# An encoder layer on one core: gt1 multiplied into the output weights ahead of the output projection, the second norm's 1/rms on ScalarE, two blocks of these weights kept, the last transposes two blocks earlier

## The chip, the cores and the metric

The kernel runs on one core of a Trainium2 chip. The metric is the device time of one execution in microseconds (us). Before the change three runs took 1608.18, 1610.39 and 1611.52 us; their median is 1610.39. The core's engines are TensorE (PE; its weight loads are shown as PEld), VectorE (DVE), ScalarE (ACT), GpSimd (POOL) and SyncE (SP). SP issues the DMAs; "SPq" in the profile is its queue. Each engine works through its own list of instructions in order, and the engines wait for one another through semaphores.

## The reference

One layer of an encoder on 1024 tokens of width 1024, in float32:

```python
h = rms_norm(x, g_norm1) * (1.0 + sc1) + sh1
proj = h @ w_in                       # q, k, v of two branches, and the gates
...                                   # neighbourhood attention -> o_a, dilated attention -> o_b
gate_a, gate_b = split(sigmoid(gates + b_gate))
merged = gate_a * (o_a @ w_proj_a) + gate_b * (o_b @ w_proj_b)
x = x + gt1 * (merged @ w_o)

h2 = rms_norm(x, g_norm2) * (1.0 + sc2) + sh2
a, up = split(h2 @ w_ffn_in)
x = x + gt2 * ((silu(a) * up) @ w_ffn_out)
```

Here `rms_norm(x, g) = x * rsqrt(mean(x*x) + eps) * g`. The six rows sh1, sc1, gt1, sh2, sc2, gt2 (1024 numbers each, the same for all tokens) come from the conditioning vector, `silu(c) @ w_ada + b_ada`. The change works on the line with gt1, on the norm behind it and on the start of the FFN. As gt1 scales columns, `gt1 * (merged @ w_o)` is also `merged @ (w_o * gt1)`.

## The kernel before

**Arithmetic.** Each float32 operand of a large matmul is split into two float32r parts, hi (a copy on ScalarE) and lo (the operand minus hi, a subtraction on GpSimd or VectorE). Three matmul passes (`PASS`: hi·hi, hi·lo, lo·hi) make one product. A matmul covers 128 x 128 x 512. So each weight tile of 128 x 512 costs a load, an ACT copy (`whi`, line 101) and a subtraction (`wlo`, line 102).

**Rings.** All weights go through `raw`, a ring of 6 buffers of 256 KB, filled by `wload` (line 94) from SP's queue. `wsplit` (lines 97 to 103) turns a raw buffer into one buffer of each of the rings `hi` and `lo`, 10 each. A buffer of a ring is filled again when all readers of its last content are done, and SP, which issues loads and stores in one list, stands at an instruction until that is so.

**Stages** (times in the profiled run): projection and attention to about 640 us; gates and merge, 641 to 829; output projection, 829 to 936; FFN in, 936 to 1400; FFN out, to the end.

*Gates and merge* (lines 882 to 900). Eight column blocks i. `gates(i, br)` makes the two sigmoid gates of a block (96 matmuls, weights `wg`), `merge(i)` the two projections and `mg = gate_a*pa + gate_b*pb` (36 matmuls, weights `wpa`, `wpb`; the VectorE lines 837 to 839). The gates of blocks 0 to 3 are already there when the loop starts, so merges 0 to 3 run back to back from 669 to 708 us, and from then on gates(i) and merge(i) take turns. In the same loop `w2_combos(k)` prepares the later FFN-out weights: four loads (`in_w` in the profile's names, which leave digits out), four dependent additions or subtractions, two on GpSimd and two on VectorE (lines 875 to 878), and four stores to DRAM (line 880, `w_d<-raw`). `W2C` says after which merge which of them are written. They use the same six raw buffers.

*Output projection* (lines 968 to 985, `SWEEPS`). Three sweeps, over the token tiles 0 to 2, 3 to 5 and 6, 7. A sweep goes over eight k blocks; for each block both halves of `wo` are loaded and split, `m` (hi and lo of the merged block, lines 963 and 964) is made, and 18 (12 in the last sweep) matmuls run. Operands are made two steps ahead (`AHEAD`). After a sweep's last block `o_post(t)` works on each tile: VectorE multiplies the product by the row gt1 (line 927) and adds it to x (line 930); ScalarE squares it with a sum (line 931); `rstd` (lines 108 to 118) makes 1/rms by ScalarE's Ln and Exp and a correction step in small VectorE operations (lines 933, 113, 115, 116, 117); VectorE scales the tile (line 935) and GpSimd adds sh2 (line 936). `o_turn(t)` (lines 939 to 950) transposes the tile on TensorE and splits it to `h2T`, the operand of the FFN. The turns of a sweep's tiles are written into the next sweep (`TK`), those of tiles 6 and 7 behind ffn1(HT, 0).

*Start of FFN in* (lines 1116 to 1130). `ffn1(j, hf)` is 48 matmuls into two PSUM banks. Four of them run first, (0,0), (HT,0), (0,1), (HT,1). The other blocks are made in pairs with seven products instead of eight (p1 to p7); for that `make_t` (lines 1036 to 1050) prepares sums and differences of `h2T` for all tiles, mostly on VectorE. p1, p2 and p3 of the first pair need no result of make_t; p6 is the first that does.

**What sets the order.** TensorE's order is the program's. For ScalarE, VectorE, GpSimd and SP the order after the start of the kernel is set by a scheduler from the program's dependences and its own costs; so an instruction that is added in one place can shift those of other lines.

## Time and profile before

| | before |
|---|---|
| median of 3 runs | 1610.39 us |
| profiled execution, of it the span | 1611.13 us, 1609.3 us |
| TensorE busy | 1549.1 us (96%), 8240 matmuls |
| VectorE, ScalarE, GpSimd busy | 1026.0, 667.0, 719.5 us |
| mean granted TensorE clock | 0.984 |
| merges 0 to 3 | 669.0 to 708.3 us |
| gates and merges 4 to 7 | to 829.1 |
| o sweeps 1, 2, 3 | to 861.6, 901.5, 935.6 |
| ffn1(0,0), ffn1(HT,0), turns 6 and 7 | to 960.9 |
| ffn1(0,1), ffn1(HT,1) | to 983.1 |
| p1, p2, p3 and p6 of the first pair | to 1010.4 |

A line of a timeline gives the start, the length, the engine, the line of the code, the operation, output and inputs by name (numbers left out), shapes, and how many instructions follow each other; behind it, in brackets, the idle time of the engine ahead of it and what ended that. A line of the windows gives, for each stretch of time, its length, the busy time and number of instructions of each engine, the granted clock of TensorE, the busy share of the 16 DMA engines and what they moved (GB/s). A line of the waits gives who waited for whom, the sum in us, how often, and the longest.

### The profile page before, as it was taken

The page shows a single profiled execution, that of the slowest core. Times are in us where ns is not written, and L with a number is a line of the kernel's source. Part 1 is how long each engine was busy: PE and PEld are TensorE (multiplying, and loading weights), DVE is VectorE, ACT ScalarE, POOL GpSimd, SP SyncE. Part 2 cuts the span into 40 slices and gives each one's busy share as a digit, 9 for nine tenths or more (in the row PEclk, how much of TensorE's full clock was granted, in tenths as well). Part 3 has the DMA queues.
Part 4 walks back from the last instruction along what each step waited for, and adds up shares of the span by engine and source line. Part 5 has one row for each costly group of instructions (what it writes and reads, how often), then busy time and mean ns, then how long its engine had stood idle before and what let it go on. Part 6 is the DMA issues. An engine that isn't in the chain of part 4 may idle for free.

```text
span 1609.3 us, 24779 instructions
## 1 busy us (share of the span) xinstructions
PE 1549.1 (96%) x8240; PEld 1293.8 (80%) x8240; DVE 1026.0 (64%) x2188; ACT 667.0 (41%) x1734; POOL 719.5 (45%) x672
## 2 busy tenths in 40 slices
PE   7989999999999999999999986999999999999997
PEld 6888888898888877878887775788888888888886
DVE  5666666776889843352437979866666666345476
ACT  5555555555545443512124533323233333344442
POOL 1332321221101040645425576867766666555565
PEclk8999999999999999999999998999999999999999
DMA  8332331344344351776645521333333333576774
GB/s 316 105 119 58 102 110 49 119 133 113 91 133 127 91 172 57 257 236 218 216 152 183 176 93 40 102 111 102 108 109 99 105 98 120 178 232 193 249 216 166
DMA packets 149056, 227.52 MB, mean 141 GB/s; under 512 B 27312, under 2 KB 65072, under 8 KB 148928
## 3 DMA queue, kind: packets, MB, share of 16 engines
q1 hardware_dynamic: 148928, 225.94, 44.1%
q8 instruction: 65, 1.06, 0.3%
q14 instruction: 63, 0.52, 0.1%
HBM read 172.28 MB, written 53.59 MB: 140 GB/s over the span
## 4 chain that ended last, share of the span: by engine, by line
PE 76%; DVE 11%; DMA 5%; issue 3%; ACT 2%; POOL 2%; SPq 0%; POOLq 0%; DVEq 0%; ACTq 0%
PE ps_d L281 14%; PE ps_t L1059 6%; PE ps_v L1059 6%; PE ps_s L1059 6%; PE ps_d L1059 6%; PE ps_d L570 4%; PE ps_d L592 4%; PE ps_s L570 4%; PE ps_d L1161 3%; PE ps_s L1161 3%; PE ps_v L473 2%; PE ps_s L432 2%; PE ps_v L1161 2%; PE ps_t L1161 2%; PE ps_t L570 2%
## 5 line engine op out<-in xcount | busy, mean ns | idle before, releaser
L102 POOL TENSOR_TENSOR wlo<-raw,whi 128x512 fp32r<-128x512 f32 (+2 forms) x269 | 362.2, 1354 | 474.9 <-ACT whi L101 455.4
L101 ACT ACTIVATE whi<-raw 128x512 fp32r<-128x512 f32 (+2 forms) x418 | 244.1, 604 | 431.3 <-DMA raw<-in_wg_dram 69.7
L281 PE MATMUL ps_d<-whi,hT 128*128 128x384 f32 x1152 | 317.9, 344 | 0.0
L102 DVE TENSOR_TENSOR wlo<-raw,whi 128x512 fp32r<-128x512 f32 (+1 forms) x149 | 150.5, 1019 | 129.0 <-ACT whi L101 114.9
L281 PEld LDWEIGHTS ps_d<-whi,hT 128*128 128x128 f32 x1152 | 211.2, 189 | 5.5 <-ACT vs L319 3.5
L281 PE MATMUL ps_d<-wlo,hT 128*128 128x384 f32 x576 | 194.2, 337 | 0.8 <-POOL wlo L102 0.8
L281 PEld LDWEIGHTS ps_d<-wlo,hT 128*128 128x128 f32 x576 | 108.9, 189 | 1.5 <-POOL wlo L102 1.5
L311 POOL TENSOR_TENSOR ra<-qn,rtab 128x64 f32<-128x64 f32 x48 | 16.5, 344 | 166.6 <-DVE qn L304 122.8
L996 POOL TENSOR_TENSOR c<-c 128x512 f32<-128x512 f32 x40 | 64.6, 1617 | 51.8 <-DVE c L1109 45.5
L101 ACT ACTIVATE whi<-ws 128x512 fp32r<-128x512 f32 x60 | 37.9, 632 | 117.1 <-DVE ws L1069 34.4
L447 ACT ACTIVATE P<-P,st 128x256 f32<-128x256 f32 (+2 forms) x100 | 46.3, 463 | 69.8 <-DVE st L446 69.8
L1059 PE MATMUL ps_t<-t,whi 128*128 128x512 f32 x160 | 52.6, 410 | 13.3 <-DVE c L995 12.1
L302 DVE TENSOR_REDUCE ss<-sq 128x4 f32<-128x256 f32 x80 | 33.2, 415 | 47.7 <-ACT sq L299 47.5
L447 ACT ACTIVATE P<-P,sx 128x384 f32<-128x384 f32 (+1 forms) x64 | 37.1, 580 | 51.6 <-DVE sx L446 51.6
L473 PE MATMUL ps_v<-PT,v 128*64 128x128 f32 (+1 forms) x672 | 55.0, 284 | 1.6 <-DVE PT L462 1.6
L458 PE MATMUL ps_t<-ident,P 128*128 128x128 f32 (+1 forms) x336 | 51.8, 275 | 4.3 <-DVE P L450 1.8
L432 PE MATMUL ps_s<-qk 64*128 64x256 f32 (+3 forms) x492 | 53.7, 321 | 2.2 <-DVE st L446 1.6
L592 PE MATMUL ps_d<-hT,whi 128*128 128x512 f32 x176 | 55.5, 396 | 0.0
L995 DVE TENSOR_TENSOR c<-c 128x512 f32<-128x512 f32 x40 | 45.5, 1139 | 14.2 <-ACT c L994 14.2
L570 PE MATMUL ps_s<-hT,whi 128*128 128x512 f32 x176 | 54.4, 390 | 0.0
L432 PEld LDWEIGHTS ps_s<-qk 64*128 64x128 f32 (+1 forms) x492 | 35.0, 182 | 24.0 <-issue 11.5
L876 DVE TENSOR_TENSOR raw<-raw 128x512 f32<-128x512 f32 x11 | 7.8, 708 | 70.9 <-DMA raw<-in_w_dram 51.4
(360 smaller groups left out, 4052.2 us busy)
## 6 DMA issues: line engine op xcount, KB each, us to landing
raw<-in_w_dram SPq DMA_DIRECT2D x165, 256.0 KB
ga_d<-c SPq DMA_DIRECT2D x77, 256.0 KB
raw<-ga_d SPq DMA_DIRECT2D x77, 256.0 KB
wa<-in_wada_dram SPq DMA_DIRECT2D x32, 512.0 KB
raw<-in_wqkv_dram SPq DMA_DIRECT2D x80, 192.0 KB
raw<-in_wo_dram SPq DMA_DIRECT2D x48, 256.0 KB
w_d<-raw SPq DMA_DIRECT2D x44, 256.0 KB
raw<-w_d SPq DMA_DIRECT2D x44, 256.0 KB
```

Source lines behind the costliest of these rows:

```text
L101: nc.scalar.activation(hi[:, :n], r, AF.Copy)
L102: (eng or nc.gpsimd).tensor_sub(lo[:, :n], r, fview(hi[:, :n]))
L281: nc.tensor.matmul(pd[:, :384], tok(a, k, t), U.w[k][b][:, :384], start=(k == 0 and i == 0), stop=(k == KT - 1 and i == 2))
L432: nc.tensor.matmul(I.pS[h][:nq, :nk], U.qk[a][hs, I.q0:I.q0 + nq], U.qk[2 + b][hs, I.kb0 * 128:I.kb0 * 128 + nk], start=(i == 0), stop=(i ...
L447: nc.scalar.activation(P[:nq, :nk], P[:nq, :nk], AF.Exp, scale=-1.0, bias=nm, accum_out=sm)
L458: nc.tensor.transpose(pt[:, i * 128:i * 128 + nq], P[:nq, i * 128:(i + 1) * 128], ident[:nq, :nq])
L473: nc.tensor.matmul(po[hs, :nq], U.v[:, I.kb0 + i, hs], I.PT[h][:, i, :nq], start=(i == 0), stop=(i == nkb - 1))
L570: nc.tensor.matmul(pb, wsl[a][:, j * 128:(j + 1) * 128], src[b][:, ksrc + j, hs], start=(done == 0 and j == 0 and i == 0), stop=(done + j ...
L592: nc.tensor.matmul(st["p"], gw[i, br][j][a][:, kk * 128:(kk + 1) * 128], hT[b][:, k, hs], start=(k == 0 and q == 0), stop=(k == 7 and q == 2))
L996: nc.gpsimd.tensor_mul(sg, sg, up) if j not in (0, HT) else nc.vector.tensor_mul(sg, sg, up)
L1059: nc.tensor.matmul(pb, w[p][:, k * 128:(k + 1) * 128], b[q][:, k], start=(k == 0 and i == 0), stop=(k == 3 and i == 2))
L1161: nc.tensor.matmul(pb[m], o[0][a][:, m * 128:(m + 1) * 128], o[1][b], start=(k == 0 and i == 0), stop=(k == HT - 1 and i == 2))
```

## The change

- **Scaled weights.** `wo_scale(hf, k)` loads a 128 x 512 block of wo through the raw ring, multiplies it in place by a broadcast row of gt1 (on GpSimd for even k, on VectorE for odd k) and stores it to a DRAM buffer `wo_d`. Sixteen such blocks are spread over the merge loop by `WOS`. The row is a tile of 128 x 512, loaded anew for the second half. The sweeps load from `wo_d` instead of `wo`.
- **o_post.** The multiply by gt1 is gone; VectorE adds the product from PSUM to x. ScalarE squares the whole tile in one operation, and the whole of 1/rms, with the correction step, is made by seven operations on ScalarE. The subtraction, scaling and GpSimd's addition behind it stay.
- **Residents.** The splits of k blocks 0 and 1 (`RES`) are made once, in tiles of their own in the pool `wo` (which takes the place of the merge stage's pool `o`), and used in all three sweeps. For these the lo part of the second half is made on VectorE.
- **Turns.** o_turn(6), o_turn(7), and the release of pools behind them, are written between ffn1(0,0) and ffn1(HT,0); the weights of the first pair and make_t follow behind ffn1(HT,0).
- Small: `c32` is put in a tile of the attention pool, `g2row` shares the `tm` buffers, and a constant 1.5 is added.

Three places show how this moves the instructions of the engines (line numbers of each version's own code; those of the changed one are higher).

SP's list before, from the weights of the merges 2 or later to the first weights of gates(4) (`in_wg`); `in_w` are the loads and `w_d` the stores of w2_combos:

```order
L94 DMA raw<-in_wpa_dram 128x512
L94 DMA raw<-in_wpb_dram 128x256
L880 DMA w_d<-raw 128x512 x2
L94 DMA raw<-in_w_dram 128x512
L880 DMA w_d<-raw 128x512
L94 DMA raw<-in_w_dram 128x512 x3
L94 DMA raw<-in_wg_dram 128x512 x2
```

and after the change the same stretch, with the loads of wo, the stores to wo_d and a load of gt1:

```order
L96 DMA raw<-in_wpb_dram 128x256
L897 DMA wo_d<-raw 128x512
L96 DMA raw<-in_w_dram 128x512
L894 DMA gt_9619<-mod_d 128x512
L96 DMA raw<-in_w_dram 128x512 x3
L96 DMA raw<-in_wo_dram 128x512 x2
L885 DMA w_d<-raw 128x512 x2
L897 DMA wo_d<-raw 128x512 x2
L96 DMA raw<-in_wo_dram 128x512
L885 DMA w_d<-raw 128x512
L96 DMA raw<-in_wg_dram 128x512
```

From the first of merge 0's weights to the first `in_wg` there were 26 ring loads and 12 stores; now there are 37 and 25.

ScalarE's list before, from the end of the merge stage (line 821 is the sigmoid of the gates) into the first o sweep:

```order
L963 ACTIVATE m<-mg 128x384
L821 ACTIVATE mg<-ps_d,cp 128x512
L821 ACTIVATE sb<-ps_s,cp 128x512
L101 ACTIVATE whi<-raw 128x512 x2
L821 ACTIVATE sb<-ps_s,cp 128x512
L916 ACT_TABLE_LOAD
L963 ACTIVATE m<-mg 128x384
L101 ACTIVATE whi<-raw 128x512 x2
```

and after, where `wr` are the resident hi parts:

```order
L826 ACTIVATE sb<-ps_s,cp 128x512
L103 ACTIVATE whi<-raw 128x512
L998 ACTIVATE m<-mg 128x384
L826 ACTIVATE sb<-ps_s,cp 128x512
L936 ACT_TABLE_LOAD
L103 ACTIVATE whi<-raw 128x512 x2
L988 ACTIVATE wr_10522<-raw 128x512
L988 ACTIVATE wr_10528<-raw 128x512
L988 ACTIVATE wr_10538<-raw 128x512
L988 ACTIVATE wr_10544<-raw 128x512
L998 ACTIVATE m<-mg 128x384
```

The copies for the first two k blocks now stand behind the last sigmoid and behind two copies for a later block; before they were among the `whi` copies ahead of it.

VectorE's list before, behind the first sweep (ss, rv, rz, ry belong to 1/rms, tm to the scaling of a tile):

```order
L933 TENSOR_TENSOR ss<-ss_10812 128x1
L113 TENSOR_SCALAR rv<-ss 128x1
L115 TENSOR_TENSOR rz<-ry,rv 128x1
L113 TENSOR_SCALAR rv<-ss 128x1
L116 SCALAR_TENSOR_TENSOR rz<-rz,ry 128x1
L117 SCALAR_TENSOR_TENSOR ry<-rz,ry 128x1
L935 SCALAR_TENSOR_TENSOR tm<-xt,ry,sc_10445 128x1024
L115 TENSOR_TENSOR rz<-ry,rv 128x1 x2
L964 TENSOR_TENSOR m<-mg,m 128x384
L116 SCALAR_TENSOR_TENSOR rz<-rz,ry 128x1 x2
L117 SCALAR_TENSOR_TENSOR ry<-rz,ry 128x1 x2
L935 SCALAR_TENSOR_TENSOR tm<-xt,ry,sc_10445 128x1024 x2
```

and after:

```order
L946 TENSOR_TENSOR xt<-xt,ps_s 128x512 x2
L946 TENSOR_TENSOR xt<-xt,ps_v 128x512 x2
L999 TENSOR_TENSOR m<-mg,m 128x384 x2
L957 SCALAR_TENSOR_TENSOR tm<-xt,rs_10810,sc_10514 128x1024
L957 SCALAR_TENSOR_TENSOR tm<-xt,rs_10829,sc_10514 128x1024
L957 SCALAR_TENSOR_TENSOR tm<-xt,rs_10848,sc_10514 128x1024
L104 TENSOR_TENSOR wlo<-raw,whi 128x512
```

The small operations between the additions and the scalings are no longer on VectorE.

The diff, cut to its core:

```diff
+WOS = (3, 3, 2, 3, 2, 2, 1, 0)
+RES = (0, 1)
...
+    gt1 = {}
+
+    def wo_scale(hf, k):
+
+        hs = slice(hf * 512, hf * 512 + 512)
+        if k == 0:
+            gt1[hf] = op_.tile([128, 512], F32, tag="gt1", bufs=1, name="gt1")
+            nc.sync.dma_start(gt1[hf], mod_d[hs].rearrange("(o n) -> o n", o=1).to_broadcast([128, 512]))
+        raw = wload(wo[k * 128:(k + 1) * 128, hs], 512)
+        (nc.vector if k % 2 else nc.gpsimd).tensor_mul(raw, raw, gt1[hf])
+        nc.sync.dma_start(wo_d[k * 128:(k + 1) * 128, hs], raw)
+
+    scaled = [(hf, k) for hf in range(2) for k in range(KT)]
...
         for k in W2C[i]:
             w2_combos(k)
+        for z in range(WOS[i]):
+            wo_scale(*scaled.pop(0))
...
-    for nm, off in (("gt1", 0), ("sh2", 1024), ("sc2", 2048)):
+    for nm, off in (("sh2", 1024), ("sc2", 2048)):
...
-    g2row = wop.tile(wide, F32, name="g2row")
+    g2row = wop.tile(wide, F32, tag="tm", bufs=4, name="g2row")
...
-        ss2 = wop.tile([128, 2], F32, tag="ss2", bufs=3, name="ss2")
-        ss = wop.tile([128, 1], F32, tag="ss", bufs=3, name="ss")
+        v, y, z = (wop.tile([128, 1], F32, tag=f"rs{i}", bufs=3, name=f"rs{i}") for i in range(3))
         for hf in range(2):
             hs = slice(hf * 512, hf * 512 + 512)
-            nc.vector.tensor_mul(tm[:, hs], pbs[hf], rows["gt1"][:, hs])
-        for hf in range(2):
-            hs = slice(hf * 512, hf * 512 + 512)
-            nc.vector.tensor_add(xt[:, hs], xt[:, hs], tm[:, hs])
-            nc.scalar.activation(tm[:, hs], xt[:, hs], AF.Square, accum_out=ss2[:, hf:hf + 1])
+            nc.vector.tensor_add(xt[:, hs], xt[:, hs], pbs[hf])
         nc.sync.dma_start(x2_d[t * 128:(t + 1) * 128, :], xt)
-        nc.vector.tensor_add(ss, ss2[:, 0:1], ss2[:, 1:2])
-        r = rstd(wop, D, 1, ss, "x2")
+        nc.scalar.activation(tm, xt, AF.Square, accum_out=v)
+        nc.scalar.activation(y, v, AF.Ln, scale=1.0 / D, bias=eps)
+        nc.scalar.activation(y, y, AF.Exp, scale=-0.5)
+        nc.scalar.activation(v, v, AF.Identity, scale=1.0 / D, bias=eps)
+        nc.scalar.activation(z, y, AF.Identity, scale=y)
+        nc.scalar.activation(z, z, AF.Identity, scale=v)
+        nc.scalar.activation(z, z, AF.Identity, scale=-0.5, bias=c15)
+        nc.scalar.activation(y, y, AF.Identity, scale=z)
+        r = y
...
+    wres = {}
+
+    def wo_split(hf, k):
+
+        if (hf, k) in wres:
+            return wres[hf, k]
+        raw = wload(wo_d[k * 128:(k + 1) * 128, hf * 512:hf * 512 + 512], 512)
+        if k not in RES:
+            return wsplit(raw, nc.vector if hf and k % 4 else None)
+        hi, lo = wres[hf, k] = [wop.tile([128, 512], F32R, name=f"wr{hf}{k}{z}") for z in range(2)]
+        nc.scalar.activation(hi, raw, AF.Copy)
+        (nc.vector if hf else nc.gpsimd).tensor_sub(lo, raw, fview(hi))
+        return hi, lo
+
     def wo_operands(sw, k):
         ts = SWEEPS[sw]
         n = len(ts) * 128
-        ws = [wsplit(wload(wo[k * 128:(k + 1) * 128, hf * 512:hf * 512 + 512], 512), nc.vector if hf and k % 4 else None)
-              for hf in range(2)]
+        ws = [wo_split(hf, k) for hf in range(2)]
...
-    for j, hf in ((0, 0), (HT, 0), (0, 1), (HT, 1)):
-        ffn1(j, hf)
-        if (j, hf) == (HT, 0):
-            o_turn(6)
-            o_turn(7)
-            wop.release()
-            mgp.release()
-            sp = pool("st", "right")
-            for f in glate:
-                f()
-            glate = None
-            pair_weights(first, 0)
-            pair_weights(first, 1)
-            tb = make_t()
+    ffn1(0, 0)
+    o_turn(6)
+    o_turn(7)
+    wop.release()
+    mgp.release()
+    sp = pool("st", "right")
+    for f in glate:
+        f()
+    glate = None
+    ffn1(HT, 0)
+    pair_weights(first, 0)
+    pair_weights(first, 1)
+    tb = make_t()
+    ffn1(0, 1)
+    ffn1(HT, 1)
```

9 lines of the change are left out of this document (6 added, 3 removed).

## The prediction

> **What bounds the kernel now.** I read the page first (busy times, the chain that ended last), then a table of windows cut at the borders of the program's stages, then TensorE's waits there, then the timelines of the engines that it waits for.
>
> ```profile
> PE 1549.1 (96%) x8240; PEld 1293.8 (80%) x8240; DVE 1026.0 (64%) x2188; ACT 667.0 (41%) x1734; POOL 719.5 (45%) x672
> PE 76%; DVE 11%; DMA 5%; issue 3%; ACT 2%; POOL 2%; SPq 0%; POOLq 0%; DVEq 0%; ACTq 0%
> ...
> core 0: us, PE busy (x) PEld busy (x) DVE busy (x) ACT busy (x) POOL busy (x), PEclk, DMA share, GB/s
> 669.00:708.25 39.25, 36.05 (x146) 28.02 (x145) 24.26 (x30) 4.36 (x8) 19.05 (x15) 0.96 0.73 241
> 708.25:829.06 120.81, 120.81 (x530) 99.20 (x529) 35.22 (x43) 27.10 (x46) 47.23 (x37) 1.00 0.56 181
> 861.56:901.48 39.92, 37.58 (x170) 30.49 (x168) 36.58 (x50) 19.94 (x47) 24.09 (x13) 0.96 0.56 189
> 901.48:935.63 34.15, 28.16 (x121) 22.52 (x120) 32.20 (x46) 20.25 (x49) 24.94 (x15) 0.90 0.58 191
> 983.07:1010.40 27.33, 14.05 (x50) 10.68 (x49) 26.41 (x24) 9.25 (x17) 20.58 (x13) 0.73 0.12 38
> ...
> PE ps_t L1059 <- DVE c L995: 12.1, 1, 12.1
> PE ps_t L945 <- DVE h2T L950: 5.7, 3, 4.1
> PE ps_d L979 <- DVE rv L113: 1.9, 1, 1.9
> PE ps_d L979 <- DVE m L964: 1.8, 1, 1.8
> ```
>
> TensorE is 96% busy, and a change to the other engines pays only where TensorE stands. The windows are, in order: merges 0 to 3; gates and merges 4 to 7; the second sweep of the output projection (the o sweeps; tiles 3 to 5); the third (tiles 6, 7); and the first pair products of the FFN up to the end of p6, the first product that needs make_t. From 708 to 829 TensorE never stops: 528 matmuls by the code in 120.81 us, 0.229 each. At that pace the second sweep, 144 matmuls and three turns at 0.79 us (from 934.84, quoted below, to the window's end at 935.63), needs 35.4 us and takes 39.92: **4.5 lost**. The third, 96 matmuls and three turns, needs 24.4 and takes 34.15: **9.8 lost**. In both VectorE is busy 92 to 94% of the time. p6 starts 12.1 us late behind VectorE. These three places, and what the change adds elsewhere, make the sum.
>
> ```profile
> 885.26 0.73 PE L979 MATMUL ps_d<-whi,m 128*128 128x512 f32 x2 [1.79 <-DVE m L964]
> 887.96 0.63 PE L979 MATMUL ps_s<-wlo,m 128*128 128x512 f32 x1
> 888.38 0.63 PE L979 MATMUL ps_s<-whi,m 128*128 128x512 f32 x1
> ...
> 929.50 1.16 PE L945 MATMUL ps_t<-ident,tm 128*128 128x128 f32 x8 [4.07 <-DVE h2T L950]
> 934.84 1.04 PE L945 MATMUL ps_t<-ident,tm 128*128 128x128 f32 x8
> ```
>
> A pause also costs after it has ended: behind the one of 1.79 us some eight matmuls start 0.42 us apart instead of 0.23 (887.96 to 888.38), about 1.6 us more, and the granted clock of that window is 0.96. I charge 1.6 to each new pause of over 1.5 us and credit it where one goes. The Trainium skill (TensorE: Matmul & The Clock Gate, Part 1) halves the clock only after an idle window of some 3.4 us. The row shows slow matmuls after 1.8 us, so the trace decides; by the page two of the credits in the sweeps and the charge at their start fall away, and the sum below comes out 1.6 us less good.
>
> **1. Output weights times gt1, in the merge stage (cost).** Sixteen times a 256 KB load, a multiply (8 on GpSimd, 8 on VectorE) and a 256 KB store, and two broadcast loads of gt1. The six raw buffers and SP's queue carry it. In the order of SP the first weight load of gates(4) now stands behind 11 loads and 10 stores of these in addition, and behind 3 more stores of the combinations.
>
> ```profile
> 659.76 0.38 SPq L94 DMA_DIRECT2D raw<-in_wpa_dram  x1
> 669.07 1.18 SPq L880 DMA_DIRECT2D w_d<-raw  x2
> 693.18 0.32 SPq L880 DMA_DIRECT2D w_d<-raw  x1
> 695.03 0.98 SPq L94 DMA_DIRECT2D raw<-in_wg_dram  x2
> ...
> 699.32 1.29 ACT L101 ACTIVATE whi<-raw 128x512 fp32r<-128x512 f32 x2 [8.29 <-DMA raw<-in_wg_dram]
> ...
> 700.35 3.44 POOL L102 TENSOR_TENSOR wlo<-raw,whi 128x512 fp32r<-128x512 f32 x2
> ...
> 708.09 0.62 PE L570 MATMUL ps_d<-hT,whi 128*128 128x512 f32 x2
> ```
>
> Now that load is issued at 695.03 and its split is done at 702.1 (half of the 3.44 us from 700.35); TensorE reaches gates(4) at 708.1, so there are 6.0 us to spare. How much later will the load be? From 659.76 to 695.03 SP issued 22 ring loads, 1.6 us each; 11 more at that pace is 17.6 us. Bandwidth sets the low end: the 11 loads, 13 stores and the second gt1 load, 262 KB each, are 6.6 MB, at 241 GB/s over a share of 0.73 (330 when full) 20.0 us, of which the free 27% of 35 us takes 9.5: 10.5 us. I take 15.4 (1.4 a load), near the ring's end, because with a share of 0.73 it is the ring and not the bandwidth that sets the pace, and a little under it because the added chain is one operation between load and store where the stage's other chain has four loads and four dependent operations. TensorE then waits 15.4 − 6.0 = 9.4, with the clock **−11.0 us**; ends −6.1 and −13.2. The merges before it may start later too, but that time lies inside the same wait.
>
> From gates(5) on, one turn of the loop is 30.2 us of TensorE (120.81 / 4) against 16 ring loads, 25.6 us at 1.6: hidden; if that cover goes, each us over 30.2 costs one, three times. The multiplies on VectorE stand beside 24.26 busy us of 39.25: nothing. The two gt1 loads are counted in the bytes.
>
> **2. Residents (cost at the start, gain later).** The k blocks 0 and 1 of both halves are split once into tiles of their own; 8 copies on ACT, 6 subtractions on GpSimd, 2 on VectorE and 8 loads fall away in sweeps 2 and 3. But at the start, in the order of ACT, two copies of block k=4 stand ahead of the four resident ones, and on GpSimd their two subtractions stand ahead of the first resident one.
>
> ```profile
> 828.86 0.63 ACT L101 ACTIVATE whi<-raw 128x512 fp32r<-128x512 f32 x1 [0.88 <-PE ps_v L570]
> 829.57 1.29 POOL L102 TENSOR_TENSOR wlo<-raw,whi 128x512 fp32r<-128x512 f32 x1 [9.80 <-ACT whi L101]
> ```
>
> Now these rows wait for the end of merge(7), and nothing hangs on them: the sweep starts at 829.06 without a gap. Afterwards the first product needs what stands behind them: the second subtraction ahead ends at 830.86 as now, the first resident low part 1.29 later at 832.2, and TensorE has one matmul to do until then: 3.1 us and the clock, **−4.7 us** (ends 0, if the copies of k=4 find their buffers free earlier, and −6: one more subtraction of 1.29).
>
> **3. o_post (gain in sweeps 2 and 3).**
>
> ```profile
> 871.89 1.31 DVE L115 TENSOR_TENSOR rz<-ry,rv 128x1 f32<-128x1 f32 x2
> 875.82 1.31 DVE L116 SCALAR_TENSOR_TENSOR rz<-rz,ry 128x1 f32<-128x1 f32 x2
> 882.50 2.71 DVE L964 TENSOR_TENSOR m<-mg,m 128x384 fp32r<-128x384 f32 x1
> ...
> 931.83 0.69 DVE L927 TENSOR_TENSOR tm<-ps_d,gt 128x512 f32<-128x512 f32 x1 [1.88 <-PE ps_d L979]
> 936.37 4.08 DVE L930 TENSOR_TENSOR xt<-xt,tm 128x512 f32<-128x512 f32 x3
> ```
>
> Off VectorE go two gt1 multiplies a tile (0.69 each by row 931.83) and the five small operations; the pairs at 871.89 and 875.82 took 1.31 each, so for three tiles 4.1 us and, by these 2.6 and my estimate of 1.5 for the other eleven, 4 us. With one resident subtraction less it is about 9 of the 36.58 and of the 32.20 busy us. The adds L930 stay, now with PSUM as an operand; from SBUF three took 4.08 us, the PSUM form of L927 0.69. I take 0.69, with 1.36 as the upper bound. The Trainium skill (SBUF — State Buffer, Who interferes with whom) says the same: a VectorE operation with two SBUF inputs is blocked by a GpSimd one that reads SBUF, one with at most one is not. By it the gt1 multiplies now on GpSimd would stop VectorE's merges too; there VectorE has 15 us free, so the sum is the same.
>
> On ACT each tile has one Square of 1024 instead of two of 512, and seven small operations instead of two. Bound for one small operation: 0.28 and 0.18.
>
> ```profile
> 912.37 0.28 ACT L112 ACTIVATE ry<-ss,eps 128x1 f32<-128x1 f32 x1
> 912.55 0.18 ACT L114 ACTIVATE ry<-ry 128x1 f32<-128x1 f32 x1
> ```
>
> Five more at 0.18 to 0.28 are 3 to 4 us for three tiles beside 20 of 34 to 40 busy us, less the 8 copies of 0.6: hidden, and no longer mixed with VectorE's queue. If that cover goes, whi copies behind them come late by as much. In sweep 2 the late m of 882.50 comes 9 us earlier, and the pause of 1.79, the smaller ones and the slow matmuls go: **+4.0** of the 4.5 (ends 2, 4.5). In sweep 3 the pauses of 1.9 and 4.07 go, but tile 5 still needs its GpSimd add (row 946.75 below: 3.05 each) when TensorE reaches its turn 9 us sooner: **+7.0** of the 9.8 (ends 3, 9.8).
>
> **4. Turns 6 and 7 ahead of ffn1(HT,0) (gain).** Let F be the start of ffn1(0,0), 935.63 now; one ffn1 is 11.0 us (48 x 0.229).
>
> ```profile
> 946.75 6.11 POOL L936 TENSOR_TENSOR tm<-tm,sh 128x1024 f32<-128x1024 f32 x2 [1.96 <-DVE tm L935]
> ...
> 959.61 1.16 PE L945 MATMUL ps_t<-ident,tm 128*128 128x128 f32 x8 [1.07 <-DVE h2T L950]
> ...
> 962.11 0.68 DVE L1040 TENSOR_TENSOR c<-h2T,h2T 128x512 f32<-128x512 f32 x1
> 1003.03 0.67 DVE L995 TENSOR_TENSOR c<-c,ps_t 128x512 f32<-128x512 f32 x1
> 1006.63 2.84 DVE L1049 TENSOR_TENSOR t<-c,t 128x512 fp32r<-128x512 f32 x2
> ...
> 1003.76 1.22 PE L1059 MATMUL ps_t<-t,whi 128*128 128x512 f32 x2 [12.14 <-DVE c L995]
> 1009.53 0.79 PE L1059 MATMUL ps_t<-t,whi 128*128 128x512 f32 x1 [1.14 <-DVE t L1049]
> ```
>
> Now tile 7 is ready for its turn at 952.9 (F+17.2), the turns come behind ffn1(HT,0) (the second at 959.61), and VectorE works on make_t from 962.11 (F+26.5) without rest to 1009.5 (F+73.9), 47.4 us, with two releases for p6: the bank at 1003.7, the last operand at 1009.5. After the change TensorE stands at the turns at F+11. The multiplies being gone, VectorE's adds end near F+3.5, ACT's chains of both tiles near F+7.5, and GpSimd's two adds (3.05 each) run from about F+8.5 to F+14.5: TensorE waits some 3.5 us there and 1.6 for the clock, last turn over at F+15.3, make_t from F+16.6 (the 1.3 us that now lie between the last transpose's end, 960.77, and 962.11), its end 47.4 later at F+64.0 instead of F+73.9. TensorE by itself would be through p6 at F+11+3.5+1.6+1.6+33+8.2+2.7 = F+61.6, so VectorE still ends it and the 5.1 us of wait lie under that cover. Gain 9.9, taken as **+9.5** since VectorE has the silu of ffn1(HT,0) inside make_t; ends 5 (tile 7 ready 4 us later) and 13.3 (TensorE's own end).
>
> **5. Small moves.** c32 in an attention tile and g2row in a tm tile change no order in the attention stage; c15 is one memset at the start: nothing, covered by the first loads.
>
> **Sum.** −11.0 − 4.7 + 4.0 + 7.0 + 9.5 = +4.8 us. The profiled run took 1611.13 (span 1609.3 and 1.8 around it): 1606.3. The median of 1610.39 is 0.7 below it, so **1605.6**. No change is anything within 0.2%, 3.2 us, about what a measurement of this kernel can tell.
>
> **Rivals.**
> - *The ring is slower (slower than before).* Between 669.07 and 693.18, where stores stand among the loads, SP issued 11 ring loads in 24.1 us, 2.2 each. The added loads are of that kind, with stores on the same queue. At 2.2 they move gates(4)'s weights by 24.1 us, the wait is 18.1 and 1.6: net −3.9, 1614.3. Break-even lies at a wait of 14.2 us (20.2 us later, 1.84 a load). Against it: a buffer of a combination waits for three others. 0.17.
> - *The moved turns give nothing (slower).* TensorE stands in order: if GpSimd's splits of the FFN weights go ahead of its adds for tiles 6 and 7 (932.17 to 952.9 it is nearly always busy), the turns come near F+22 as now. Then net 4.8 − 9.5 = −4.7, 1615.1; it decides once less than 4.7 us of the gain is left. Against it: 6 subtractions fewer in the sweeps before. 0.14.
> - *The ring hides it.* At the low end of part 1 the wait is 4.5 us and 1.6: net +9.7, 1600.7; each load that SP issues earlier still takes off more. For it: a DMA share of 0.73 and an added chain of one operation. 0.22.
> - *The sweeps do not gain.* ACT's chains hold up the whi copies as VectorE's did: 2 us of the 11 left, net −4.2, 1614.6. For it: sweep 3 has three chains of eight operations in 24 us. 0.08.
>
> **Numbers.** The forecast has 0.39, with a range of its own of 1599 to 1612. Of it 0.28 is faster, 0.09 the same, 0.02 slower; of the three slow rivals (0.39 together) about 0.27 slower, 0.08 the same, 0.04 faster; the hidden ring is faster. Faster 0.54, same 0.17, slower 0.29. The range 1593 to 1617 runs from the hidden ring with the upper ends of parts 3 and 4 (7.1 more: 1593.6) to the slow ones with 2 us more.
>
> **What would show it.** A pause of TensorE before the first gates(4) matmul that ends on the split of in_wg, near 9 us (part 1); one of 3 us at the first matmul of the o sweeps behind GpSimd's first resident subtraction (2); windows of the sweeps of 36 and 27 us with VectorE's share down by 9 us (3); a wait of a few us at turns 6 and 7, and p6 ending at F+65 (4). Wrong it is if gates(4) starts without a gap or over 14 us late, or if the pause before p6 stays over 8 us.

## The result and the profile after

The changed kernel is **slower**: 1620.53 us as the median of six runs (1613.28 to 1622.93) against 1610.95 for the kernel before in six runs beside it; the ratio is 1.0059, with a 95% interval of 1.0039 to 1.0079. The forecast was 1605.6, a gain of 0.3%, with a range up to 1617. The profiled execution took 1619.78 us, span 1618.0; before it was 1611.13 and 1609.3.

From the starts of TensorE's stages in both timelines the 8.7 us of span can be placed. Here and in the later tables each column is a duration in us, and the stages follow each other; "to gates(4)" begins with the first matmul of merge 0, "sweeps 1+2" begins at the end of merge(7), so it holds a pause at their start, "FFN start" runs from ffn1(0,0) to the end of p6. The differences are those of the unrounded times.

| kernel | ahead of merge 0 | to gates(4) | gates(4) to merge(7) | sweeps 1+2 | sweep 3 | FFN start | rest | span |
|---|---|---|---|---|---|---|---|---|
| before | 668.9 | 39.2 | 120.8 | 72.6 | 34.1 | 74.9 | 598.8 | 1609.3 |
| changed | 667.8 | 52.8 | 123.0 | 73.5 | 32.7 | 67.8 | 600.5 | 1618.0 |
| difference | −1.0 | +13.6 | +2.1 | +0.9 | −1.4 | −7.2 | +1.7 | +8.7 |

Two views of the changed kernel say what stands behind this. First the windows at the same borders (in order: merges 0 to 3 with the wait behind them; gates and merges 4 to 7 with the first pause of the sweeps; the three sweeps), then TensorE's waits from 630 to 1025 us.

```profile
core 0: us, PE busy (x) PEld busy (x) DVE busy (x) ACT busy (x) POOL busy (x), PEclk, DMA share, GB/s
667.80:720.62 52.82, 35.05 (x145) 26.41 (x143) 26.76 (x36) 3.31 (x6) 21.82 (x18) 0.91 0.82 272
720.62:844.57 123.95, 122.81 (x529) 99.97 (x529) 34.74 (x47) 29.60 (x50) 51.93 (x42) 0.98 0.61 201
844.57:881.39 36.82, 34.81 (x145) 28.27 (x145) 16.00 (x20) 11.29 (x21) 10.63 (x8) 0.95 0.54 193
881.39:917.04 35.65, 35.65 (x169) 29.51 (x168) 29.03 (x28) 19.39 (x55) 19.53 (x10) 1.00 0.54 182
917.04:949.90 32.86, 26.89 (x122) 21.30 (x121) 24.07 (x22) 18.59 (x51) 26.09 (x15) 0.95 0.51 171
...
PE ps_d L575 <- ACT whi L103: 13.6, 1, 13.6
PE ps_d L1014 <- DVE m L999: 4.8, 1, 4.8
PE ps_t L575 <- DVE mg L843: 4.2, 4, 1.9
PE ps_t L967 <- DVE h2T L972: 2.6, 2, 2.0
PE ps_t L967 <- POOL tm L958: 2.5, 1, 2.5
PE ps_d L1014 <- POOL wr L989: 2.0, 1, 2.0
PE ps_t L1094 <- DVE c L1030: 2.0, 1, 2.0
PE ps_d L1014 <- ACT wr L988: 1.0, 1, 1.0
```

The old waits are gone: p6's 12.1 us is 2.0, the second sweep runs at TensorE's pace (35.65 us, all of it busy, where it took 39.92). In their place stand four new ones: 13.6 us before gates(4), 3.0 us at the start of the sweeps, 4.8 us in the third sweep, 2.5 and 2.0 us at the turns. The waits on VectorE inside the merges (4.2 us together) were there before too (3.2 us).

The largest, in SP's, ScalarE's and TensorE's timelines of the changed kernel, with the first matmul of merge 0:

```profile
688.69 4.31 SPq L885 DMA_DIRECT2D w_d<-raw  x3
715.50 0.38 SPq L96 DMA_DIRECT2D raw<-in_wg_dram  x1
...
719.94 0.63 ACT L103 ACTIVATE whi<-raw 128x512 fp32r<-128x512 f32 x1 [13.91 <-DMA raw<-in_wg_dram]
...
667.83 0.62 PE L575 MATMUL ps_t<-oT,whi 128*128 128x512 f32 x2
...
720.62 1.22 PE L575 MATMUL ps_d<-hT,whi 128*128 128x512 f32 x2 [13.61 <-ACT whi L103]
```

and merge 0's first matmul in the kernel before:

```profile
668.86 0.63 PE L570 MATMUL ps_t<-oT,whi 128*128 128x512 f32 x2
```

The first weight of gates(4) is issued at 715.50 instead of 695.03, 20.5 us later. But merge 0 itself began 1.0 us sooner than before, at 667.83 instead of 668.86. Counted from there the load comes 21.5 us later for 11 more ring loads: 1.95 each. Stores among the loads hold SP's list up (the three from 688.69 were 4.31 us in issuing). TensorE starts as soon as the hi part is copied, so it waits from 707.0, the end of merge(3), to 720.6.

### The profile page after: what moved, and what is told of

It reads as the page before. It is cut to its first block, busy times and chain, and to the rows that moved or that the text cites. A ratio compares the mean times of both kernels' runs of the same rounds, so it can differ in the third digit from the quotient of the medians.

```text
span 1618.0 us, 24779 instructions
## 1 busy us (share of the span) xinstructions
PE 1548.9 (96%) x8240; PEld 1292.1 (80%) x8240; DVE 1011.1 (62%) x2140; ACT 663.6 (41%) x1750; POOL 720.4 (45%) x673
## 4 chain that ended last, share of the span: by engine, by line
PE 75%; DVE 9%; DMA 6%; POOL 3%; ACT 3%; issue 3%; SPq 0%; POOLq 0%; DVEq 0%; ACTq 0%
PE ps_d L286 13%; PE ps_d L1094 6%; PE ps_t L1094 6%; PE ps_s L1094 6%; PE ps_v L1094 6%; PE ps_d L597 4%; PE ps_s L575 3%; PE ps_d L575 3%; PE ps_d L1197 3%; PE ps_s L1197 3%; PE ps_v L1197 2%; PE ps_s L437 2%; PE ps_t L1197 2%; PE ps_v L478 2%; PE ps_d L1014 2%
## 5 line engine op out<-in xcount | busy, mean ns | idle before, releaser
L104 POOL TENSOR_TENSOR wlo<-raw,whi 128x512 fp32r<-128x512 f32 (+2 forms) x260 | 348.3, 1347 | 481.8 <-ACT whi L103 477.3
L103 ACT ACTIVATE whi<-raw 128x512 fp32r<-128x512 f32 (+2 forms) x406 | 236.0, 603 | 377.2 <-DMA raw<-in_wg_dram 64.0
L104 DVE TENSOR_TENSOR wlo<-raw,whi 128x512 fp32r<-128x512 f32 (+1 forms) x146 | 155.4, 1073 | 132.8 <-ACT whi L103 122.9
L103 ACT ACTIVATE whi<-ws 128x512 fp32r<-128x512 f32 x60 | 37.8, 630 | 150.2 <-DVE ws L1104 84.1
L316 POOL TENSOR_TENSOR ra<-qn,rtab 128x64 f32<-128x64 f32 x48 | 16.4, 342 | 166.6 <-DVE qn L309 122.6
L1031 POOL TENSOR_TENSOR c<-c 128x512 f32<-128x512 f32 x40 | 66.3, 1659 | 54.3 <-DVE c L1144 50.5
L452 ACT ACTIVATE P<-P,st 128x256 f32<-128x256 f32 (+2 forms) x100 | 46.3, 463 | 69.3 <-DVE st L451 69.2
L575 PE MATMUL ps_d<-hT,whi 128*128 128x512 f32 x160 | 50.6, 398 | 13.6 <-ACT whi L103 13.6
L1103 DVE TENSOR_TENSOR ws<-raw 128x512 f32<-128x512 f32 x20 | 24.4, 1220 | 59.5 <-POOL wlo L104 50.8
L597 PE MATMUL ps_d<-hT,whi 128*128 128x512 f32 x176 | 55.5, 396 | 0.0
```

What stands on the lines that cost most here:

```text
L103: nc.scalar.activation(hi[:, :n], r, AF.Copy)
L104: (eng or nc.gpsimd).tensor_sub(lo[:, :n], r, fview(hi[:, :n]))
L452: nc.scalar.activation(P[:nq, :nk], P[:nq, :nk], AF.Exp, scale=-1.0, bias=nm, accum_out=sm)
L575: nc.tensor.matmul(pb, wsl[a][:, j * 128:(j + 1) * 128], src[b][:, ksrc + j, hs], start=(done == 0 and j == 0 and i == 0), stop=(done + j ...
L597: nc.tensor.matmul(st["p"], gw[i, br][j][a][:, kk * 128:(kk + 1) * 128], hT[b][:, k, hs], start=(k == 0 and q == 0), stop=(k == 7 and q == 2))
L1031: nc.gpsimd.tensor_mul(sg, sg, up) if j not in (0, HT) else nc.vector.tensor_mul(sg, sg, up)
```

## Experiments

All kernels of a group ran on one chip beside the kernel before, whose median was 1608.4 in the first group, 1608.86 in the second, 1611.03 in the third and 1611.65 in the last. Ratios are to those. The changed kernel's own ratio of 1.0059 is the yardstick; it comes from the result and was not measured again in these groups.

The stages of the profiled execution of each, as in the table above:

| kernel | to gates(4) | gates(4) to merge(7) | sweeps 1+2 | sweep 3 | FFN start | rest | ratio to before (95%) |
|---|---|---|---|---|---|---|---|
| changed | 52.8 | 123.0 | 73.5 | 32.7 | 67.8 | 600.5 | 1.0059 (1.0039 to 1.0079) |
| wos_late | 36.3 | 127.8 | 73.5 | 32.4 | 66.6 | 599.5 | 0.9979 (0.9966 to 0.9992) |
| res_45 | 54.3 | 123.8 | 68.5 | 27.4 | 66.8 | 600.1 | 1.0008 (0.9995 to 1.0021) |
| turns_old | 53.5 | 123.0 | 73.5 | 32.1 | 76.5 | 596.8 | 1.0092 (1.0077 to 1.0108) |
| rstd_dve | 54.8 | 123.0 | 73.0 | 32.0 | 60.3 | 598.8 | 1.0016 (1.0006 to 1.0027) |
| combo | 37.2 | 127.7 | 68.5 | 29.0 | 66.8 | 600.2 | 0.9932 (0.9910 to 0.9953) |
| combo_dve | 38.8 | 127.2 | 68.0 | 26.1 | 67.8 | 601.1 | 0.9911 (0.9892 to 0.9930) |
| before_turns | 38.2 | 120.8 | 75.0 | 34.1 | 67.5 | 600.0 | 0.9986 (0.9972 to 0.9999) |
| nraw8 | 38.5 | 125.9 | 73.5 | 30.6 | 63.7 | 593.7 | one run, 1596.45 us |
| res_none | 51.3 | 123.7 | 71.4 | 29.1 | 65.7 | 599.0 | 1.0020 (1.0005 to 1.0034) |
| before_n8 | 33.9 | 120.8 | 73.3 | 35.3 | 75.4 | 596.3 | 0.9966 (0.9954 to 0.9978) |
| combo_n8 | 37.3 | 120.7 | 69.3 | 27.1 | 67.7 | 594.1 | 0.9820 (0.9801 to 0.9839) |
| combo_n8_dve | 35.0 | 120.7 | 69.3 | 27.6 | 68.2 | 593.7 | 0.9831 (0.9816 to 0.9846) |
| opost_alone | 38.9 | 120.7 | 72.7 | 30.3 | 75.0 | 595.7 | 0.9932 (0.9912 to 0.9951) |
| opost_res01 | 38.3 | 120.9 | 73.4 | 32.5 | 76.0 | 595.5 | 0.9970 (0.9955 to 0.9985) |

Ahead of merge 0 the profiled executions lie between 664.8 and 673.1 us, although that part is nearly the same code in all of them; a span differs by some of this by chance, and the ratios of several runs carry the verdicts.

### The scaling behind gates(4): wos_late

```diff
-WOS = (3, 3, 2, 3, 2, 2, 1, 0)
+WOS = (0, 0, 0, 0, 5, 5, 5, 1)
```

> The changed kernel with WOS = (0, 0, 0, 0, 5, 5, 5, 1): no output weight is scaled before gates(4), all sixteen are scaled in the turns i = 4 to 7. Theory (the ring in front of gates(4)): the first weight load of gates(4) is issued near 695 us again instead of 715.5, the wait of 13.6 us and the slow matmuls behind it (1.6) go, and the five extra loads a turn stay hidden under 30 us of TensorE: about 1605, 15 below the changed kernel. Rival (the extra transfers and multiplies cost wherever they are): the stall only moves to gates(5) to gates(7), 4 to 5 us each, and the time stays within 4 us of the changed kernel, 1617 or more.

Measured: 1605.04 us, ratio 0.9979. The wait before gates(4) is gone, and 13 us of the changed kernel's time with it (1.0059 less 0.9979 is 0.8%). The stretch to gates(4) takes 36.3 us, even less than before. It is not free: gates and merges 4 to 7 take 127.8 us instead of 123.0 (120.8 in the kernel before), with two of the waits that the rival spoke of, though smaller than its 4 to 5:

```profile
766.38 0.93 PE L575 MATMUL ps_d<-hT,whi 128*128 128x512 f32 x2 [2.36 <-ACT whi L103]
...
799.70 0.73 PE L575 MATMUL ps_d<-hT,whi 128*128 128x512 f32 x2 [0.86 <-ACT whi L103]
```

With 5 extra loads a turn of 30 us the ring was too tight there too: my "hidden" for the later turns holds for the two extra that the change has, not for five.

### A larger ring: nraw8 and before_n8

```diff
-NRAW, NHL = 6, 10
+NRAW, NHL = 8, 9
```

> The changed kernel with eight raw buffers and nine of hi and lo each (NRAW, NHL = 8, 9) instead of six and ten; the same loads and stores. Theory (the number of raw buffers sets the pace in front of gates(4): 1.86 us for each added load at six buffers): the pace is 6/8 of it, and the wait before gates(4) falls from 13.6 us to 5 or less. Rival (the DMA engines set the pace, whose share was 0.82 in that stretch): the wait stays at 10 us or more.

> The kernel before with NRAW, NHL = 8, 9 and nothing else. Theory (in the kernel before the ring holds up nothing in the merge stage; what it gains lies behind p6): merges and sweeps as before within 2 us, the rest 4 to 6 us shorter, 0.2 to 0.4% faster than before, about 1605. Rival (nine hi and lo buffers cost the sweeps what eight raw ones gain): within 0.1% of before.

nraw8 is the changed kernel with this, before_n8 the kernel before. In nraw8 the 13.6 us became 4.8 and, for the lo part, 2.9 more:

```profile
668.75:707.30 38.55, 33.76 (x145) 26.84 (x143) 24.53 (x33) 3.31 (x6) 18.39 (x15) 1.00 0.91 305
...
707.30 0.87 PE L575 MATMUL ps_d<-hT,whi 128*128 128x512 f32 x2 [4.79 <-ACT whi L103]
711.10 0.80 PE L575 MATMUL ps_d<-hT,wlo 128*128 128x512 f32 x1 [2.93 <-POOL wlo L104]
```

The same loads and stores moved at 305 GB/s instead of 272, over a DMA share of 0.91 instead of 0.82, once there were more buffers. The hi and lo rings were one buffer smaller, so the gain is not theirs. So the number of raw buffers sets the pace in the changed kernel. Counted from the start of merge 0, the first in_wg load is issued after 31.5 us here and after 16.9 in before_n8: 1.33 for each of the 11 loads, where six buffers gave 1.95. With eight the DMA engines may be the next limit; no run tries that. The wait that is left, 7.7 us in two pieces, lies between the two expectations; TensorE also got there sooner, since the merges ahead of it took 33.8 us instead of 39.2.

before_n8 gained 0.34%. I had expected that in the kernel before the ring holds up nothing ahead of gates(4); that is wrong. Its merges 0 to 3 took 33.9 us instead of 39.2, TensorE busy throughout, so the small waits on VectorE's merges in the kernel before (1.86 us the longest) went with the larger ring as well. The rest behind p6 was 2.4 us shorter instead of the 4 to 6 expected, sweep 3 1.2 us longer.

### Other kept blocks, or none: res_45 and res_none

```diff
-RES = (0, 1)
+RES = (4, 5)
```

(res_none has `RES = ()`.)

> The changed kernel with RES = (4, 5): k blocks 4 and 5 are kept instead of 0 and 1, so that as many splits are saved in sweeps 2 and 3, but the first sweep begins with ordinary splits. Theory (the copies of the resident blocks stand behind the end of merge(7)): the pauses of 1.0 and 2.0 us at the start of the first sweep and the slow matmuls go, the first sweep takes 33 instead of 38 us: about 1615.5. Rival (the start is late because the scaled weights come back late from DRAM, or because merge(7) ends late): the start of the sweep still waits 3 us, about 1620.

> The changed kernel with RES = (): no k block is kept, every sweep loads and splits all of them. Theory (blocks 0 and 1 kept save work in sweep 3 where VectorE stands idle anyway, and cost the start of the first sweep 5 us): the start's pauses go, sweeps 1 and 2 together take 68 to 69 us (changed kernel 73.5), sweep 3 stays within 2 us of 32.7: 3 to 5 below the changed kernel, about 1616. Rival (the splits saved are worth what they cost at the start, wherever they lie): sweeps 2 and 3 lose 4 us or more, and the time is that of the changed kernel or above.

Measured: 1608.8 (1.0008) and 1612.13 (1.0020). The start's pauses are gone in both. But the third sweep fell too, from 32.7 us to 27.4 with blocks 4 and 5, and to 29.1 with none at all. So keeping blocks 0 and 1 did not only cost at the start; the third sweep was slower with them than without. I had no such term. With none kept, sweeps 1 and 2 took 71.4 us instead of the 68 to 69 expected: TensorE stood 3.0 us at a turn in the second.

### o_post by itself, and with blocks 0 and 1 kept

```diff
-WOS = (3, 3, 2, 3, 2, 2, 1, 0)
-RES = (0, 1)
+WOS = (0, 0, 0, 0, 0, 0, 0, 0)
+RES = ()
...
-        raw = wload(wo_d[k * 128:(k + 1) * 128, hf * 512:hf * 512 + 512], 512)
+        raw = wload(wo[k * 128:(k + 1) * 128, hf * 512:hf * 512 + 512], 512)
```

with the turns in their old place; opost_res01 has `RES = (0, 1)`. No weight is scaled in either, and the multiply by gt1 is left out.

> The kernel before with o_post of the changed kernel alone: no weight is scaled (WOS all 0, the sweeps load wo itself), RES = (), old place of the turns. The multiply by gt1 is left out altogether, so the time is that of the sweeps with 1/rms on ScalarE and the addition from PSUM. Theory (part 3 by itself takes VectorE's 9 us out of the way): sweeps 1 and 2 together 69 us (before 72.6), sweep 3 27 to 29 (before 34.1), merges as before: 8 to 10 below before, about 1601. Rival (the new chain on ScalarE takes most of it back): sweep 3 at 32 or more, 2 to 4 below before.

> The kernel opost_alone with RES = (0, 1), without the scaled weights and the traffic of the merge stage (the multiply by gt1 is left out here too). Theory (blocks 0 and 1 kept cost by themselves, at the start by the copies behind merge(7), and in sweep 3 since VectorE idles at its start and is crowded at its middle): sweeps 1 and 2 together 73 to 74 us, sweep 3 32 to 33: 6 to 9 above opost_alone. Rival (they cost only together with the late weights of the changed kernel's merge stage): within 2 us of opost_alone.

opost_alone took 1599.46, ratio 0.9932: an o_post without VectorE's multiplies and small operations is worth 0.7%. Of this the sweeps gave 3.7 us, all in sweep 3 (34.1 to 30.3); sweeps 1 and 2 took 72.7 as before. Another 3.1 us came behind p6, for which I have no mechanism. The profiled execution was the slowest of the four (1603.20), so some 4 us of the gain are not placed. With blocks 0 and 1 kept the time rose to 1606.62 (0.9970), 7.2 us more, without any of the changed kernel's merge stage. Of these, 0.7 and 2.2 us lie in the sweeps and 1.0 at the FFN start; in the profiled execution the rest lies ahead of merge 0, which the blocks do not touch. So the 6 to 9 us of my theory came out in the time, but only 2.9 of them in the sweeps, the place that it named. The waits of the changed kernel's sweeps are there again, to a few hundredths of a us:

```profile
910.47 0.42 DVE L999 TENSOR_TENSOR m<-mg,m 128x256 fp32r<-128x256 f32 x1 [2.11 <-ACT m L998]
914.32 0.69 DVE L104 TENSOR_TENSOR wlo<-raw,whi 128x512 fp32r<-128x512 f32 x1 [3.42 <-ACT whi L103]
917.56 5.65 DVE L957 SCALAR_TENSOR_TENSOR tm<-xt,rs,sc 128x1024 f32<-128x1024 f32 x2
923.13 2.84 DVE L104 TENSOR_TENSOR wlo<-raw,whi 128x512 fp32r<-128x512 f32 x1
925.89 2.56 DVE L999 TENSOR_TENSOR m<-mg,m 128x256 fp32r<-128x256 f32 x1
...
833.27 0.49 PE L1014 MATMUL ps_d<-wr,m 128*128 128x512 f32 x1 [1.00 <-ACT wr L988]
835.77 1.65 PE L1014 MATMUL ps_d<-wr,m 128*128 128x512 f32 x3 [2.01 <-POOL wr L989]
928.50 1.22 PE L1014 MATMUL ps_d<-whi,m 128*128 128x512 f32 x2 [4.76 <-DVE m L999]
```

This is how, by these lines, blocks 0 and 1 hurt the third sweep. At its start VectorE stands idle, 2.1 and 3.4 us, waiting for ScalarE's copies; then the scalings of three tiles, a weight split and an m operand come in one piece, two scalings at 2.8 us each and a split at 2.84, while GpSimd adds and splits at the same time, and TensorE waits for the m at their end. Sparing the splits of the first two blocks takes away work where VectorE has nothing to do. With blocks 4 and 5 spared, the crowded middle is thinned out: in res_45 VectorE was busy 18.05 us in that sweep, in the changed kernel 24.07. It did not have fewer operations (23 against 22); each took less time, for instance 4.30 instead of 5.65 us for the same two scalings, beside 11 operations of GpSimd instead of 15:

```profile
917.30:944.70 27.40, 24.81 (x121) 20.33 (x120) 18.05 (x23) 18.83 (x54) 19.78 (x11) 1.00 0.58 192
```

No run moves these operations alone, so that the crowding makes the whole difference is argued, not shown.

### The correction step back on VectorE: rstd_dve

```diff
-        nc.scalar.activation(y, v, AF.Ln, scale=1.0 / D, bias=eps)
-        nc.scalar.activation(y, y, AF.Exp, scale=-0.5)
-        nc.scalar.activation(v, v, AF.Identity, scale=1.0 / D, bias=eps)
...
-        r = y
+        r = rstd(wop, D, 1, v, "x2")
```

> The changed kernel with the correction step of 1/rms on VectorE as before (Ln and Exp on ScalarE); the Square of 1024 and the addition from PSUM stay. Theory (ScalarE's 24 small operations, done for three tiles side by side, finish all tiles late: the first scaling in sweep 3 begins at 926.3, 9 us after the sweep's start): the scalings begin 5 us or more earlier, the wait of 4.75 us on m in sweep 3 goes with its slow matmuls, while sweep 2 gets 1 to 2 us of VectorE's small operations back: about 1616. Rival (VectorE's small operations were the cost of sweeps 2 and 3): sweeps 2 and 3 get back to 38 and 34 us, about 1624.

Measured: 1610.89, ratio 1.0016, 0.4% below the changed kernel. But not where the theory had it: sweep 3 took 32.0 us against 32.7, its wait on m fell to 2.92 and another of 1.87 came at a turn. What fell was the FFN start, from 67.8 to 60.3 us: ffn1(HT,0) began 14.0 us behind ffn1(0,0) instead of 19.3. So ScalarE's chains did not make sweep 3 slow; in this kernel they, or the order that the scheduler makes with them, delayed tiles 6 and 7. In combo_dve and combo_n8_dve (below) the same edit gave nothing at that place, 67.8 and 68.2 us, so it is not a cost of the chain as such. Which of the neighbours in the order makes the difference stays open.

### The place of the turns: turns_old and before_turns

```diff
+    ffn1(0, 0)
+    o_turn(6)
+    o_turn(7)
...
+    ffn1(HT, 0)
```

turns_old takes these lines back in the changed kernel, before_turns puts them into the kernel before.

> The changed kernel with the turns of tiles 6 and 7 behind ffn1(HT,0) again, as before the change. Theory (VectorE's start of make_t sets p6): p6 ends about 7 us later behind the start of ffn1(0,0), near 75 us instead of 67.7, with a pause of 9 to 12 us before it: about 1627. Rival (the shorter o_post frees the turns and make_t by itself, so that the place of the turns matters little): within 2 us of the changed kernel, 1619 to 1622.

> The kernel before with only the turns of tiles 6 and 7 (and the release of the pools) moved ahead of ffn1(HT,0). Theory (make_t's start sets p6, whatever o_post is): TensorE waits about 6 us at the turns, since tile 7 is ready 17 us after the start of ffn1(0,0), and p6 still ends 3 to 5 us earlier: 0.2 to 0.3% faster than before, about 1606. Rival (without the shorter o_post the wait at the turns eats the gain): within 0.1% of before.

In both the FFN start changes as forecast in kind: 76.5 us with the old place against 67.8 in the changed kernel (8.7), 67.5 with the new place against 74.9 in the kernel before (7.4). The whole time moves by less: turns_old is 1.0092, 0.33% (5.3 us) above the changed kernel, before_turns 0.9986, 2.2 us below before. In both pairs part of it is given back behind p6: with the early turns the rest is longer by 3.6 and 1.3 us, and TensorE stands there once more for VectorE:

```profile
950.73 1.97 PE L945 MATMUL ps_t<-ident,tm 128*128 128x128 f32 x8 [4.43 <-POOL tm L936]
...
1019.13 1.22 PE L1059 MATMUL ps_d<-h2T,whi 128*128 128x512 f32 x2 [2.31 <-DVE c L1100]
```

These are lines of before_turns; the changed kernel has the same wait at 1034.01, 2.35 us. In before_turns sweeps 1 and 2 also took 2.4 us more, with a wait of 3.3 us at a turn of the second sweep. Its gain of 0.14% lies between the theory (0.2 to 0.3%) and the rival (0.1%).

### Together: combo, combo_dve, combo_n8, combo_n8_dve

```diff
-NRAW, NHL = 6, 10
-WOS = (3, 3, 2, 3, 2, 2, 1, 0)
-RES = (0, 1)
+NRAW, NHL = 8, 9
+WOS = (1, 1, 1, 1, 4, 4, 3, 1)
+RES = (4, 5)
```

This is combo_n8; combo keeps the rings at 6 and 10 and has `WOS = (1, 1, 1, 0, 4, 4, 4, 1)`; the two with _dve have the edit of rstd_dve in addition.

> The changed kernel with both repairs: WOS = (1, 1, 1, 0, 4, 4, 4, 1) and RES = (4, 5). Theory (the wait before gates(4) and the late resident copies are two separate losses, and the rest of the change gains): merges and gates take about 162 us to the first o matmul (before 160.2), the o sweeps 96 (before 106.6), ffn1(0,0) to the end of p6 67.5 (before 74.9), and 2 us go later: 14 below before, about 1596 with before at 1610. Rival (the two repairs overlap, since each removes a pause that makes room for the same late work of VectorE and GpSimd in sweep 3): one of them gains nothing beside the other, 1602 to 1606.

> The kernel combo with the correction step of 1/rms on VectorE as before. Theory (ScalarE's chains make the tiles late, above all tiles 6 and 7, whose turns waited 2.5 to 4 us for GpSimd's addition): the wait at turns 6 and 7 falls to about 1 us and p6 comes 5 us earlier after ffn1(0,0), the sweeps stay within 2 us: about 1592 with before at 1610. Rival (with the resident blocks at 4 and 5 ScalarE has the room, and VectorE's small operations cost sweep 2 its gain): 1597 or more.

> Eight raw buffers and nine of hi and lo (NRAW, NHL = 8, 9), WOS = (1, 1, 1, 1, 4, 4, 3, 1), RES = (4, 5), all else as in the changed kernel. Theory (the larger ring helps the stages behind too: in nraw8 the part from the end of p6 took 593.7 us instead of 600): the waits of 2 to 3 us before gates(5) in combo go, the rest is 5 us shorter: about 1589 with before at 1610. Rival (ring size and the later scaling remove the same wait, and the rest's gain was one run's chance): 1594 to 1597.

> The kernel combo_n8 with the correction step of 1/rms on VectorE as before. Theory (with blocks 4 and 5 kept neither engine is short in the sweeps, so the place of seven small operations does not matter): within 2 us of combo_n8, sweeps and FFN start included. Rival (ScalarE's chains delay the tiles): 3 us or more below combo_n8, most of it between ffn1(0,0) and p6.

combo took 1596.92 (0.9932), about 1596 expected: the two repairs are separate losses and add up, the one of 0.8% and the one of 0.5%, as the theory said. combo_n8 took 1582.79, ratio 0.9820 with an interval of 0.9801 to 0.9839, and beats both kernels by far: 28 us less than before beside it. It was 6 us below what I expected. TensorE's waits in it from 660 to 1000 us:

```profile
PE ps_t L967 <- POOL tm L958: 4.1, 3, 1.9
PE ps_s L1094 <- DVE wlo L104: 2.2, 1, 2.2
PE ps_t L575 <- DVE mg L843: 1.9, 1, 1.9
PE ps_t L967 <- DVE h2T L972: 1.1, 2, 0.7
PE ps_s L1094 <- ACT whi L103: 1.1, 1, 1.1
```

None above 2.2 us is left. Where 1/rms is made does not matter once the rest is in order: combo_dve and combo overlap (0.9911 and 0.9932), and so do combo_n8_dve and combo_n8. That is the rival of combo_dve: p6 did not come 5 us sooner.

## Why the prediction was wrong

The bound and the kinds of waits were read rightly: every new pause that the prediction named appeared at its place; one more, 4.8 us in the third sweep, it did not name. The sum was wrong because three terms were mis-sized, and the net of large terms of both signs came out on the other side of no change.

**Part 1, the weights of gates(4): right in mechanism, too small.** The step that failed is "I take 15.4 (1.4 a load)". Measured from the start of merge 0 are 21.5 us, 1.95 a load. I had 1.6 from the mean pace of the ring and 2.2 from its slowest stretch, and took less than either, since one operation between load and store seemed quicker than four. But the ring is not paced by the operations alone: in SP's list an added load also stands behind the stores of others, and it holds its buffer until its own store is done. nraw8 shows that it is the buffers. The spare time was not 6.0 us but 8.1, because TensorE starts with the hi part (699.97 before, half of the 1.29 us from 699.32) and not the lo part. So two errors partly cancelled: with 6.0 to spare the wait would have been 15.5, not 13.6. The rival for a slower ring, at 0.17, had its break-even at 1.84 a load, and the run was past that; the wait stayed just under its 14.2. Wait, slow clock and the rest of the stage are 13.6 and 2.1 us, **15.7 lost where 11.0 were put down**. With the other terms as forecast that alone leaves +0.1, no change; the shortfalls of parts 2 to 4 made it slower.

**Part 2, the kept blocks: the cost at the start right, another left out.** Forecast 4.7 us at the start; the first sweep took 37.8 us from the end of merge(7) instead of 32.7, 5.2. The pauses were as forecast, 3.0 us for 3.1. What I put at nothing without a reason is their cost in the third sweep (opost_res01 against opost_alone, 2.2 us; res_none against the changed kernel, 3.6). I had counted the spared splits as lying on VectorE's busy time, from the mean share of the sweep (92 to 94%), and not looked where in the sweep they lay.

**Part 3, o_post: +7.0 for sweep 3 did not come.** It was 1.4 in the changed kernel; opost_alone shows that 3.8 were to be had without the kept blocks. For sweep 2, +4.0 was forecast and 4.3 measured (39.92 to 35.65). But the agreement is partly luck: opost_alone left sweeps 1 and 2 together at 72.7 us, with a wait of 3.0 at a turn, so in the changed kernel the kept blocks had their share in sweep 2's gain. The rival "the sweeps do not gain", at 0.08, blamed ScalarE's chains; rstd_dve does not bear that out for sweep 3.

**Part 4, the turns: right in kind, +9.5 for 7.2, and 1.7 given back.** make_t was to start at F+16.6 and started at 973.30, F+23.5:

```profile
957.10 0.69 DVE L1103 TENSOR_TENSOR ws<-raw 128x512 f32<-128x512 f32 x1 [3.86 <-DMA raw<-in_w_dram]
957.71 3.51 DVE L957 SCALAR_TENSOR_TENSOR tm<-xt,rs,sc 128x1024 f32<-128x1024 f32 x2
973.30 3.09 DVE L1075 TENSOR_TENSOR c<-h2T,h2T 128x512 f32<-128x512 f32 x5
...
960.09 6.07 POOL L958 TENSOR_TENSOR tm<-tm,sh 128x1024 f32<-128x1024 f32 x2
...
963.47 1.97 PE L967 MATMUL ps_t<-ident,tm 128*128 128x128 f32 x8 [2.51 <-POOL tm L958]
1014.66 0.73 PE L1094 MATMUL ps_t<-t,whi 128*128 128x512 f32 x2 [2.01 <-DVE c L1030]
1034.01 0.73 PE L1094 MATMUL ps_d<-h2T,whi 128*128 128x512 f32 x2 [2.35 <-DVE c L1135]
```

On VectorE a sum of FFN weights (L1103) stands ahead of the scalings of tiles 6 and 7 and waited 3.9 us for its load; I had taken the adds and the chains as the only work in front of them. GpSimd's additions then ended at 966.2 (F+16.4 instead of F+14.5), and the silu of ffn1(0,0) came before make_t. That VectorE ends p6 was right, and so were the waits at the turns (2.5 and 2.0 us, one of 3.5 forecast).

**The sum by measured terms.** −15.7 (part 1), −5.2 (start), +4.3 and +1.4 (sweeps), +7.2 and −1.7 (FFN) give −9.7; the 1.0 us by which the profiled execution reached merge 0 sooner makes it the 8.7 of the spans. The forecast for the same terms was −11.0 − 4.7 + 4.0 + 7.0 + 9.5. 10 of the 13.5 us of error lie in part 1 and sweep 3.

## What to carry to other kernels

A ring of buffers that a stage shares has a price per added load, and its mean pace understates it: here the mean was 1.6 us, the slowest stretch with stores in it 2.2, and an added load cost 1.95. What stands first in line behind the added loads pays all of it at once, so look up the next weights whose arrival TensorE waits for, and put the added work behind them. Work that is spared was worth something here only where the engine had no idle time: keep the blocks whose splits fall into the crowded part of a sweep, not those at its start. When a forecast is the small net of large terms of both signs, its chances should be near even, and the parts should be tried apart: here all four, with other settings and a larger ring, were worth 1.8%, where the larger ring alone gave the kernel before 0.3%.
